# New costs in a planner's clock, constants and product order set anew, and the RG-LRU gate weights loaded once per layer: a two-layer hybrid diffusion backbone on one Trainium2 core

## The chip, the core and the metric

The kernel runs on one core of one Trainium2 chip, as one launch. The metric is the device time of that launch in microseconds, median of the runs. One execution was also taken by the hardware profiler; its span runs from the first to the last instruction. Engines in the rows: PE is TensorE (matmuls), PEld its weight loads, DVE is VectorE, ACT is ScalarE, POOL is GpSimd, SP is SyncE, which here only issues DMAs (SPq is its queue).

## What is computed

Two trunk layers over 128 context tokens and 512 latent tokens of width 1024, all fp32. Each layer is a modulated RMSNorm, one input projection that feeds three parallel mixers, an output projection, a second modulated RMSNorm and a gated MLP of width 2816. Cut to what matters here:

```python
def mixer(h, states, p, pos):
    proj = h @ p['w_in']                       # q k v g | z xbc dt | xl gl
    ...                                        # (A) retention, 6 heads, both directions
    xbc = jax.nn.silu(dwconv(xbc, ...))        # (B) Mamba-2 SSD, 6 heads, both directions
    dt_f = jax.nn.softplus(dt_raw + p['ssd_dt_bias'][0])
    ...
    xl = dwconv(xl, p['lru_conv_w'], p['lru_conv_b'])    # (C) RG-LRU, 256 channels
    def lru_dir(xd, d, h0):                    # d = 0 forwards, 1 backwards
        r = sigmoid(xb @ p['lru_w_a'][d] + b)  # block-diagonal gate weights
        i = sigmoid(xb @ p['lru_w_x'][d] + b)
        log_a = -LRU_C * r * softplus(-p['lru_lambda'][d])
        return rglru_scan(log_a, i * xd, h0)
    out = concatenate([y_ret, y_ssd, y_lru]) @ p['w_out']

def conv_ffn(h, p):
    u = dwconv(h @ p['ffn_w_up'], ...)         # width-3 depthwise
    val, gate = split(u, 2)
    return (silu(gate) * val) @ p['ffn_w_down']
```

The outputs are the tokens after a last RMSNorm and the final context states of the three scans.

## The kernel before

**Tiles.** The 640 tokens are five tiles of 128 (tile 0 is the context). The normalised input lies feature-major in `h_hi` and `h_lo`, 8 blocks of 128 features by 642 columns (two zero columns part context and latents). Each fp32 product is three passes over split operands: high by high, high by low, low by high (names `wh`, `wl` for the weight's parts). A feature-major unit is one weight tile of 128x1024 (`raw`, split by ACT into `wh` and by DVE or POOL into `wl`): 8 blocks by 3 passes by two column pieces of 258 and 384, 48 matmuls. Token-major sweeps (`v`, `q`, `k`, `z`, output and down projections) take units of 30 matmuls.

**Order.** Everything is written by one program that plays a scheduler while it emits. A main stream of jobs (the products, in the order of a string such as `'l0 v l1 c6 ...'`) runs beside cooperative threads (convolutions, scans, retention, SSD, norms, modulation). `Clock` holds an estimated time for each engine; `Engine.account` adds an estimated cost for each instruction as it is emitted; a thread is stepped when its inputs should be there by that clock. The estimate sets nothing but the order: each engine then executes its own list in that order, and waits on the chip for whatever is late. `TUNE` holds four sets of constants (mixer and MLP of layer 0, mixer and MLP of layer 1): the order string, `look` (how many weight units are split ahead of the product that takes them), `bias` (how early each kind of thread is stepped), `stages` (below) and others.

**The RG-LRU gates.** For each layer there are two channel blocks c and two directions d. `lru` loads the 128x2x128 gate weights of one (c, d) into a tile `wg` that has one buffer, and multiplies them by the convolved input `X`: two kinds (r and i), two pieces each, four fp32 matmuls `at<-X,wg`. So there are eight loads, and each one but the first of a layer must wait for the last matmul of the one before; the load stands in SP's queue wherever the thread came to it, often right behind the store of the last direction's state (`out_lru`), which waits for a DVE scan:

```python
            wg = fb.tile([128, 2, 128], F32, tag="wg", name="wg")
            SP.dma_start(wg, a["wlru"][l, c, :, d])
            yield 1
```

**Stages.** At the start of an MLP, and of layer 1's mixer, the first two or three units (`fm_primed`) run while the norm still turns the last tiles. They take the columns in parts: "A" is 0:258, 258:386, 386:642; "B" is 0:258, 258:642; "C" is 0:258, 258:514, 514:642.

**The start.** `start` loads x, norms it (ACT square and root, DVE reciprocal and scaling), transposes it on PE into PSUM, copies it into `xT`, while `setup` runs a softplus of some 25 small DVE instructions (`sp`, `lg`, `lam`, `e`); then `part` adds the bias to the first modulation's `rows`, PE transposes them, and `feats` scales `xT` and splits it into `h_hi` and `h_lo` for the first products.

Of the kernel before, what the change touches and what calls it, by code (L numbers as in the profile page):

```python
# [28 lines left out]
    {'look': 2, 'cap': 2.5, 'keep': 5, 'npr': 3, 'pmore': '', 'cf': 3, 'kz': 7, 'ke': 7, 'el': 5, 'order': 'l0 v l1 c6 c5 c3 c2 c4 q gl1 k z gl0', 'backlog': 4.9, 'slack': 1.53, 'lobias': 1.5, 'plag': 2.7, 'pbonus': 5.8, 'mkeep': 0, 'ng': 0, 'fine': 0, 'stages': 'B', 'bias': {'ret_chain': -0.2, 'ssd_run': 5.2, 'outs': 4.2, 'ret_tables': -3.6, 'ret_run': 4.4, 'rest': 2.0, 'ssd_chain': -2.1, 'dt_run': 2.8, 'states': 3.5, 'lru_run': 4.2}, 'klast': 1},  # L29
    {'look': 1, 'cap': 2, 'keep': 8, 'npr': 2, 'pmore': '0', 'cf': 3, 'kz': 5, 'ke': 8, 'el': 4, 'order': 'v l0 c2 c3 c4 c5 c6 l1 q k z gl0 gl1', 'backlog': 6.7, 'slack': 1.99, 'lobias': 0.6, 'plag': 0.7, 'pbonus': 1.5, 'mkeep': 0, 'ng': 0, 'fine': 0, 'stages': 'A', 'bias': {}, 'klast': 1},  # L30
    {'look': 2, 'cap': 2, 'keep': 3, 'npr': 3, 'pmore': '', 'cf': 2, 'kz': 3, 'ke': 8, 'el': 4, 'order': 'v l0 c2 c6 c5 c4 c3 l1 q z gl1 k gl0', 'backlog': 5.8, 'slack': 1.0, 'lobias': 1.6, 'plag': -1.0, 'pbonus': 3.8, 'mkeep': 0, 'ng': 0, 'fine': 0, 'stages': 'C', 'bias': {'ret_tables': -1.0, 'ret_run': -1.2, 'ssd_run': -2.7, 'ret_chain': 3.8, 'dt_run': 2.6, 'ssd_chain': -1.6, 'outs': 2.3, 'rest': -2.2, 'states': 0.2}, 'klast': 2},
    {'look': 1, 'cap': 1, 'keep': 8, 'npr': 3, 'pmore': '0', 'cf': 3, 'kz': 5, 'ke': 8, 'el': 4, 'order': 'v l0 c2 c3 c4 c5 c6 l1 q k z gl0 gl1', 'backlog': 5.6, 'slack': 0.49, 'lobias': 1.0, 'plag': 0.1, 'pbonus': 4.0, 'mkeep': 0, 'ng': 0, 'fine': 1, 'stages': 'C', 'bias': {}, 'klast': 1},
# [27 lines left out]
class Clock:  # L60
    """estimated times of the engines, for the order in which instructions are emitted"""

    def __init__(self):
        self.t = {k: 0.0 for k in ("PE", "ACT", "DVE", "POOL", "SP", "DMA")}
        self.ready, self.read, self.fin = {}, {}, 0.0
        self.table, self.dep, self.last = None, 0.0, 0.0
        self.cold, self.win, self.busy, self.rows = True, 0, 0.0, 1.0

# [11 lines left out]
    def add(self, eng, cost, lat, ins, outs):  # L80
# [30 lines left out]
    def free(self, n):  # L111
        """when the last user of a tile is done"""
# [18 lines left out]
ROWS = {"xT": NT, "s0": 2, "sh0": 2, "h_hi": NT, "h_lo": NT, "C456": 384}  # L131


def tnames(xs):
    """what the waits go by: tiles, or the rows of the tiles that are worked on in parts"""
    res = []
    for x in xs:
        n = getattr(getattr(x, "tensor", x), "name", None)
        w = ROWS.get(n.rsplit("_", 1)[0]) if n else None
        if w and not n.startswith(SHARED):  # L140
            ap = [(abs(st), c) for st, c in list(x.ap)[1:]]
            o = x.offset
            res += [f"{n}#{r}" for r in range(o // w, (o + sum(st * (c - 1) for st, c in ap)) // w + 1)]
        elif tname(x):
# [4 lines left out]
class Slots:  # L149
    """a pool whose tiles take over the waits of the tiles that had their place"""  # L150
# [16 lines left out]
class Engine:  # L167
# [13 lines left out]
    def account(self, fn, args, kw):  # L181
        def size(x):
            return int(np.prod([c for c in x.shape[1:]]))
# [10 lines left out]
        ns = sum(1 for x in aps[1:] if size(x) == 1 and n > 1)  # L194
        if self.key == "PE":
            f32 = args[1].dtype == F32
            cost = n * (4 if f32 and fn == "matmul" else 1) / 2400 + 0.003
# [15 lines left out]
        elif self.key == "DVE":  # L213
            if fn == "memset":
                return
            if fn == "tensor_scalar":
                cost = n / (960 if any(map(psum, ins)) else 1920) + 0.063 * (1 + ns)
            elif fn == "scalar_tensor_tensor":
                cost = n / 960 + 0.069 + 0.06 * ns
            elif fn == "reciprocal":  # L220
# [4 lines left out]
        elif self.key == "POOL":  # L225
            cost = 0.14 + n * 0.00216
            lat = 0.15
        else:
            b = n * 4 * out.shape[0] / 360e3
            start = max(c.t["SP"], c.dep)  # L230
            names = tnames(ins), tnames(outs)
            c.add("SP", 0.475, 0, *names)
            c.t["DMA"] = max(c.t["DMA"], c.t["SP"] + 0.65) + b
            for x in names[1]:
                c.ready[x] = (c.t["DMA"] + 1.0, "DMA")
            for x in names[0]:
                c.read.setdefault(x, {})["DMA"] = c.t["DMA"] + 1.0
            return
        c.add(self.key, cost, lat, tnames(ins), tnames(outs))
# [3 lines left out]
def kernel(ctx: ExitStack, tc: tile.TileContext, a: dict, o: dict):  # L243
# [27 lines left out]
    # PSUM tiles and token-major tiles are taken and given back in emission order, so that no engine waits for a later one  # L271
# [1637 lines left out]
```

## Time and profile before

| | us |
|---|---|
| median of three runs | 1764.8 |
| lowest, highest run | 1762.87, 1765.51 |
| span of the profiled execution | 1752.2 |
| median less span (launch and end, outside the span) | 12.6 |
| PE busy in the span | 1661.6 |
| DVE, ACT, POOL busy in the span | 1009.3, 718.5, 537.4 |

The profiler gives no other time for its own execution than the span, so that execution's time is the span and what lies around it, which the runs put at 12.6 us. Busy shares are averages over stages. A wait of an engine is put down in the rows to what was released last before it went on.

### The profile page before, as it was taken

The page shows a single profiled execution, that of the slowest core. Times are in us where ns is not written, and L with a number is a line of the kernel's source. Part 1 is how long each engine was busy: PE and PEld are TensorE (multiplying, and loading weights), DVE is VectorE, ACT ScalarE, POOL GpSimd, SP SyncE. Part 2 cuts the span into 40 slices and gives each one's busy share as a digit, 9 for nine tenths or more (in the row PEclk, how much of TensorE's full clock was granted, in tenths as well). Part 3 has the DMA queues.
Part 4 walks back from the last instruction along what each step waited for, and adds up shares of the span by engine and source line. Part 5 has one row for each costly group of instructions (what it writes and reads, how often), then busy time and mean ns, then how long its engine had stood idle before and what let it go on. Part 6 is the DMA issues. An engine that isn't in the chain of part 4 may idle for free.

```text
span 1752.2 us, 25505 instructions
## 1 busy us (share of the span) xinstructions
PE 1661.6 (95%) x10192; PEld 1485.5 (85%) x10192; DVE 1009.3 (58%) x1866; ACT 718.5 (41%) x1136; POOL 537.4 (31%) x344
## 2 busy tenths in 40 slices
PE   6897999999999999999999899999899999999997
PEld 5787878768997999799789876887799989998996
DVE  5467987677443344344464779877854434443445
ACT  6466435426332233223274765443453313331333
POOL 1334653322331233123123355442213212321331
PEclk9998999999999999999999999999999999999999
DMA  8424555533223222322533355643122321222222
GB/s 326 121 49 81 128 179 174 187 109 103 73 73 108 64 82 73 96 73 73 180 121 107 75 135 158 181 166 105 60 73 73 87 81 61 73 85 72 73 85 84
DMA packets 62668, 188.63 MB, mean 108 GB/s; under 512 B 9550, under 2 KB 17734, under 8 KB 62550
## 3 DMA queue, kind: packets, MB, share of 16 engines
q1 hardware_dynamic: 62550, 187.01, 34.7%
q8 instruction: 80, 1.31, 0.3%
q14 instruction: 38, 0.31, 0.1%
HBM read 180.46 MB, written 6.52 MB: 107 GB/s over the span
## 4 chain that ended last, share of the span: by engine, by line
PE 72%; DVE 14%; ACT 4%; DMA 4%; issue 3%; POOL 1%; SPq 0%; POOLq 0%; DVEq 0%; ACTq 0%
PE at L175 72%; DVE tok L175 5%; DVE x L175 2%; DMA wg<-in_wlru 2%; DVE gt L175 1%; DVE sp L175 1%; DVE C L175 1%; DMA tok<-cTd 1%; ACT L175 1%; DVE lb L175 1%; ACT xn L175 1%; ACT hf L175 1%; POOL wl L175 1%; DMA araw<-in_w_ada 1%; ACT lb L175 1%
## 5 line engine op out<-in xcount | busy, mean ns | idle before, releaser
L175 POOL TENSOR_TENSOR wl<-raw,wh 128x1024 fp32r<-128x1024 f32 (+3 forms) x167 | 388.3, 2326 | 946.7 <-ACT wh L175 883.2
L175 PE MATMUL at<-h_hi,wh 128*128 128x258 f32 (+2 forms) x1912 | 599.9, 314 | 5.0 <-ACT wh L175 3.9
L175 PE MATMUL at<-h_hi,wl 128*128 128x258 f32 (+2 forms) x1912 | 590.4, 309 | 5.6 <-POOL wl L175 4.8
L175 PE MATMUL at<-h_lo,wh 128*128 128x258 f32 (+2 forms) x1912 | 590.0, 309 | 0.5 <-DVE h_lo L175 0.5
L175 PEld LDWEIGHTS at<-h_hi,wh 128*128 128x128 f32 x1912 | 363.7, 190 | 20.1 <-issue 5.2
L175 PEld LDWEIGHTS at<-h_hi,wl 128*128 128x128 f32 x1912 | 362.8, 190 | 6.9 <-POOL wl L175 5.9
L175 PEld LDWEIGHTS at<-h_lo,wh 128*128 128x128 f32 x1912 | 364.1, 190 | 2.6 <-DVE h_lo L175 0.7
L175 ACT ACTIVATE wh<-raw 128x1024 fp32r<-128x1024 f32 (+3 forms) x210 | 212.7, 1013 | 223.1 <-PE at L175 168.1
L175 DVE SCALAR_TENSOR_TENSOR cv<-at,par,cv 128x258 f32<-128x258 f32 (+1 forms) x352 | 185.9, 550 | 71.4 <-ACT cv L175 59.6
L175 ACT ACTIVATE cv<-at,par 128x258 f32<-128x258 f32 (+1 forms) x130 | 76.5, 601 | 317.4 <-PE at L175 317.4
L175 PE MATMUL at<-wh,h_hi 128*128 128x384 f32 (+2 forms) x480 | 184.9, 385 | 2.3 <-DVE tok L175 1.4
L175 PE MATMUL at<-wl,h_hi 128*128 128x384 f32 (+2 forms) x480 | 172.6, 359 | 2.7 <-POOL wl L175 2.7
L175 PE MATMUL at<-wh,act_hi 128*128 128x512 f32 x440 | 174.3, 396 | 0.0
L175 PE MATMUL at<-wl,act_hi 128*128 128x512 f32 x440 | 173.6, 395 | 0.6 <-POOL wl L175 0.6
L175 PE MATMUL at<-wh,act_lo 128*128 128x512 f32 x440 | 173.4, 394 | 0.0
L175 PE MATMUL at<-wh,h_lo 128*128 128x384 f32 (+2 forms) x480 | 172.5, 359 | 0.0
L175 DVE TENSOR_SCALAR cv<-at,par 128x384 f32<-128x384 f32 x46 | 31.2, 677 | 188.3 <-PE at L175 188.3
L175 DVE TENSOR_TENSOR gt<-at,gate 128x512 f32<-128x512 f32 x100 | 68.4, 684 | 104.2 <-PE at L175 104.2
L175 ACT ACT_TABLE_LOAD x87 | 111.6, 1283 | 21.9 <-PE at L175 13.6
L175 PEld LDWEIGHTS at<-wh,h_hi 128*128 128x128 f32 x480 | 91.3, 190 | 28.4 <-issue 12.6
L175 PEld LDWEIGHTS at<-wh,act_hi 128*128 128x128 f32 x440 | 82.7, 188 | 24.0 <-issue 3.4
L175 PEld LDWEIGHTS at<-wl,h_hi 128*128 128x128 f32 x480 | 91.2, 190 | 12.2 <-POOL wl L175 3.5
(169 smaller groups left out, 1903.1 us busy)
## 6 DMA issues: line engine op xcount, KB each, us to landing
raw<-in_wup SPq DMA_DIRECT2D x88, 512.0 KB, 3.5
araw<-in_w_ada SPq DMA_DIRECT2D x80, 512.0 KB, 4.5
raw<-in_wdn SPq DMA_DIRECT2D x44, 512.0 KB, 3.5
raw<-in_wfm SPq DMA_DIRECT2D x28, 512.0 KB, 3.6
ar<-in_wada SPq DMA_DIRECT2D x16, 512.0 KB, 10.2
tok<-cTd SPq DMA_DIRECT2D x40, 192.0 KB, 4.6
raw<-in_wout SPq DMA_DIRECT2D x14, 512.0 KB, 3.5
x<-in_xin SPq DMA_DIRECT2D x10, 512.0 KB
```

Of the source, the lines that this page charges most:

```text
L175: res = real(*args, **kw)
```

## The change

It has five parts.

1. **Clock and costs.** Matmul costs, DVE's scan and the landing of a DMA get other numbers; tiles that many threads share (`h_hi`, `h_lo`, `act_hi`, `act_lo`) are now tracked by rows and blocks of columns; and DVE and POOL instructions that both read SBUF take turns in the clock (`port`). None of this emits an instruction; it changes the order.
2. **Constants.** All four sets of `TUNE`. Among them: `stages` C to A for layer 1's mixer, A to B and C to B for the MLPs; `look` 2 to 1 for layer 1's mixer and 1 to 2 for the last MLP; `lobias` down in the last MLP, which moves low-part splits from POOL to DVE.
3. **Product order** of both mixers (`v` first in layer 0; `z` ahead of `k`).
4. **Gate weights.** `wg` is one tile of 128x2x2x2x128 per layer, loaded by two DMAs when the pool `fb` is opened.
5. Comments and docstrings go.

```diff
-    {'look': 2, ..., 'order': 'l0 v l1 c6 c5 c3 c2 c4 q gl1 k z gl0', ..., 'stages': 'B', ...},
+    {'look': 2, ..., 'order': 'v l0 l1 c6 c5 c4 c3 c2 q z k gl1 gl0', ..., 'stages': 'B', ...},
...
+    def port(self, eng, start, cost):
+        other = self.held["POOL" if eng == "DVE" else "DVE"]
+        for a, b in other:
+            if a <= start < b:
+                start = b
+        mine = self.held[eng]
+        mine.append((start, start + cost))
+        if len(mine) > 24:
+            del mine[0]
+        return start
...
+        if port:
+            start = self.port(eng, start, cost)
...
-ROWS = {"xT": NT, "s0": 2, "sh0": 2, "h_hi": NT, "h_lo": NT, "C456": 384}
+ROWS = {"xT": NT, "s0": 2, "sh0": 2, "h_hi": NT, "h_lo": NT, "act_hi": NT, "act_lo": NT, "C456": 384}
...
             if fn == "transpose":
                 cost = 0.109
-            tp = kw.get("tile_position")
-            if tp is not None and tp[1] > 0:
-                cost = 0.02
+            elif args[1].dtype != F32:
+                cost = max(0.112, 0.0055 + 0.000443 * n)
+            elif tp is not None:
+                cost = 0.108 if args[1].shape[1] == 64 else 0.32 if n == 512 else 0.1
+            else:
+                cost = 2 * max(0.111, 0.00084 * n)
...
+            land = c.t["DMA"] + (3.4 if wide else 1.4)
             for x in names[1]:
-                c.ready[x] = (c.t["DMA"] + 1.0, "DMA")
+                c.ready[x] = (land, "DMA")
...
         for d in range(2):
             gates = []
-            wg = fb.tile([128, 2, 128], F32, tag="wg", name="wg")
-            SP.dma_start(wg, a["wlru"][l, c, :, d])
+            wg = mods["wg", l][:, c, d]
             yield 1
...
         def lru_run(c):
-            while c > len(st["lru"]):
+            while c > len(st["lru"]) or ("wg", l) not in mods:
                 yield
...
                     pl.enter("fb", f"fb{l}")
+                    wg = mods["wg", l] = pl["fb"].tile([128, 2, 2, 2, 128], F32, tag="wg", name="wg")
+                    for c in range(2):
+                        SP.dma_start(wg[:, c], a["wlru"][l, c])
                     S["C456"] = pl["fb"].tile([128, 3 * NT], F32, tag="C456", name="C456")
```

What this does to the engines' lists, at three places. First SP's queue in layer 0's mixer (each row a DMA, tile<-source, width; `raw` is a weight unit, `araw` a modulation unit). Before:

```order
L175 DMA wg<-in_wlru 128x256
L175 DMA raw<-in_wfm 128x1024 x2
L175 DMA out_lru<-Y 128x1
L175 DMA wg<-in_wlru 128x256
L175 DMA raw<-in_wfm 128x1024
L175 DMA rows<-in_bada 128x512
```

After, from the last loads of the start on:

```order
L195 DMA raw<-in_wvd 128x780 x3
L195 DMA araw<-in_w_ada 128x1024 x2
L195 DMA wg<-in_wlru 128x512 x2
L195 DMA pv<-in_sssd 128x192 x4
L195 DMA raw<-in_wvd 128x780
L195 DMA raw<-in_wfm 128x1024 x4
```

The loads of `wg` no longer stand behind `out_lru`; both of the layer stand ahead of the state loads `pv` and of the fourth `v` unit, and no load of `wg` follows in that mixer. The four groups of gate products move later: on PE, 78 main matmuls now stand between the end of `v` and the product of the log-decays `la`, where in layer 1 there were 66.

Second, PE at the start of layer 0's MLP, around the last modulation unit (`araw`) between two stages. Before:

```order
L175 MATMUL at<-h_hi,wh 128x128
L175 MATMUL at<-h_lo,wh 128x128
L175 MATMUL at<-h_hi,wl 128x128
L175 MATMUL at<-araw,csil 32x512 x4
L175 MATMUL at<-h_hi,wh 128x256
L175 MATMUL at<-h_lo,wh 128x256
L175 MATMUL at<-h_hi,wl 128x256
```

After:

```order
L195 MATMUL at<-h_hi,wh 128x258
L195 MATMUL at<-h_lo,wh 128x258
L195 MATMUL at<-h_hi,wl 128x258
L195 MATMUL at<-araw,csil 32x512 x4
L195 MATMUL at<-h_hi,wh 128x384
L195 MATMUL at<-h_lo,wh 128x384
L195 MATMUL at<-h_hi,wl 128x384
```

Pairs of a 128 and a 256 columns wide matmul have become one of 384. Over the three stage plans 120 such pairs go (48 here, 72 in the last MLP); layer 1's mixer keeps its pairs in another order.

Third, DVE in the start. Before:

```order
L175 RECIPROCAL rs<-ss 128x1
L175 TENSOR_SCALAR x<-x,rs 128x1024
L175 TENSOR_SCALAR sp_149<-sp_148 128x32
L175 RECIPROCAL sp_149<-sp_149 128x32
L175 TENSOR_TENSOR sp_148<-sp_148,sp_149 128x32
```

After:

```order
L195 TENSOR_SCALAR x<-x,rs 128x1024
L195 TENSOR_SCALAR spi<-par 128x32
L195 COPY xT<-at 128x4x128 x5
L195 TENSOR_SCALAR sp_184<-sp_183 128x32
L195 RECIPROCAL sp_184<-sp_184 128x32
L195 TENSOR_TENSOR sp_183<-sp_183,sp_184 128x32
```

Five of the ten copies of the turned x have come from ACT to DVE, ahead of the softplus chain. Further on, 39 more low-part splits of a weight (`wl`) are on DVE than before and as many fewer on POOL: 40 more in the last MLP, two more in the first, three fewer in the mixers.

## Rows read from the trace of the kernel before

**Rows 1.** The page's first part: each engine's busy time, share of the span, instructions.

```profile
PE 1661.6 (95%) x10192; PEld 1485.5 (85%) x10192; DVE 1009.3 (58%) x1866; ACT 718.5 (41%) x1136; POOL 537.4 (31%) x344
```

**Rows 2.** Busy by stretch: length, PE, PEld, DVE, ACT, POOL (instructions), granted clock, DMA share, GB/s.

```profile
412.00:870.00 458.00, 458.00 (x2781) 421.91 (x2782) 203.31 (x320) 141.19 (x192) 113.89 (x49) 1.00 0.29 93
```

**Rows 3.** PE's timeline, gate products: start, length, operation, [idle before it, releaser].

```profile
84.78 2.48 PE L175 MATMUL at<-X,wg 128*128 128x258 f32 x4 [6.94 <-DMA wg<-in_wlru]
152.29 3.98 PE L175 MATMUL at<-X,wg 128*128 128x258 f32 x7 [11.07 <-DMA wg<-in_wlru]
991.17 2.48 PE L175 MATMUL at<-X,wg 128*128 128x258 f32 x4 [6.14 <-DVE tok L175]
1033.83 1.32 PE L175 MATMUL at<-X,wg 128*128 128x258 f32 x4 [3.19 <-DMA wg<-in_wlru]
1060.59 2.48 PE L175 MATMUL at<-X,wg 128*128 128x258 f32 x4 [3.75 <-DVE tok L175]
```

**Rows 4.** The chain that ended last, two loads of wg: start, length.

```profile
141.69 10.46 DMA wg<-in_wlru
...
1025.49 8.20 DMA wg<-in_wlru
```

**Rows 5.** SP's timeline, the load of wg ahead of the product at 991.17.

```profile
983.50 0.38 SPq L175 DMA_DIRECT2D wg<-in_wlru  x1
```

**Rows 6.** DVE's timeline, the instruction that ended as PE went on at 991.17.

```profile
990.78 0.28 DVE L175 TENSOR_SCALAR tok<-cst,dt 128x128 f32<-128x128 f32 x1
```

**Rows 7.** Busy by stretch, as rows 2: during gate waits and just after.

```profile
84.80:90.00 5.20, 5.20 (x13) 4.21 (x14) 0.00 (x0) 1.62 (x4) 0.00 (x0) 0.50 0.30 104
...
141.20:152.30 11.10, 0.03 (x2) 0.04 (x1) 5.95 (x14) 5.06 (x5) 2.80 (x1) 0.65 0.76 38
152.30:158.30 6.00, 6.00 (x15) 4.42 (x16) 0.00 (x0) 2.87 (x6) 0.70 (x1) 0.51 0.22 82
...
985.00:991.20 6.20, 0.06 (x2) 0.06 (x1) 5.91 (x14) 2.17 (x3) 0.96 (x1) 0.71 0.55 38
991.20:994.50 3.30, 3.30 (x9) 2.51 (x10) 1.34 (x5) 1.27 (x3) 0.00 (x0) 0.50 0.54 201
1056.80:1060.60 3.80, 0.05 (x2) 0.04 (x1) 3.73 (x11) 0.01 (x1) 2.74 (x3) 0.83 1.25 46
1060.60:1066.20 5.60, 5.60 (x13) 4.40 (x14) 3.53 (x11) 1.38 (x3) 1.65 (x1) 0.50 0.83 314
```

**Rows 8.** PE's timeline, first and last of runs 256 and 128 columns wide, at full clock.

```profile
907.10 0.28 PE L175 MATMUL at<-h_lo,wh 128*128 128x256 f32 x1
...
912.60 0.28 PE L175 MATMUL at<-h_hi,wl 128*128 128x256 f32 x1
...
912.88 0.28 PE L175 MATMUL at<-h_hi,wl 128*128 128x128 f32 x1
...
915.34 0.28 PE L175 MATMUL at<-h_hi,wh 128*128 128x128 f32 x1
```

**Rows 9.** The same for a run of 384 columns, first and last of 40.

```profile
159.16 0.34 PE L175 MATMUL at<-wh,h_hi 128*128 128x384 f32 x1
...
165.99 0.34 PE L175 MATMUL at<-wh,h_hi 128*128 128x384 f32 x1
```

**Rows 10.** PE's timeline, layer 1's product of the log-decays.

```profile
952.74 0.85 PE L175 MATMUL at<-la,cst 128*128 128x60 f32 x6 [2.12 <-DVE la L175]
```

**Rows 11.** ACT's timeline of the start, the ten copies of the turned x.

```profile
15.00 4.97 ACT L175 ACTIVATE xT<-at 128x512 f32<-128x512 f32 x10
```

**Rows 12.** DVE's timeline of the start, in the softplus chain.

```profile
20.98 2.39 DVE L175 TENSOR_SCALAR lam<-spo 128x8 f32<-128x8 f32 x2
```

**Rows 13.** POOL's timeline of the start.

```profile
20.98 2.37 POOL L175 TENSOR_TENSOR wl<-raw,wh 128x1024 fp32r<-128x1024 f32 x1 [20.54 <-ACT wh L175]
```

**Rows 14.** Groups by form: count, busy us, mean ns of one, idle before and its releasers.

```profile
L175 ACT ACTIVATE wh<-raw 128x1024 fp32r<-128x1024 f32 x174 | 183.3, 1053 | 207.8 <-PE at L175 160.4 <-DVE x L175 36.5 <-issue 5.8
...
L175 DVE TENSOR_TENSOR wl<-raw,wh 128x1024 fp32r<-128x1024 f32 x37 | 45.3, 1224 | 79.1 <-ACT wh L175 78.3
```

More of the change, by code (lines that the diff above doesn't have):

```diff
@@ L33 @@
+    {'look': 2, 'cap': 0.5, 'keep': 8, 'npr': 3, 'pmore': '0', 'cf': 3, 'kz': 5, 'ke': 8, 'el': 4, 'order': 'v l0 c2 c3 c4 c5 c6 l1 q k z gl0 gl1', 'backlog': 6.5, 'slack': -0.22, 'lobias': 0.39, 'plag': -3.5, 'pbonus': 4.0, 'mkeep': 0, 'ng': 0, 'fine': 0, 'stages': 'B', 'bias': {'dt_run': -0.4, 'load_gate': -0.5, 'ret_tables': 2.4, 'feats': 0.7, 'rest': -0.5, 'lru_fin': -2.8, 'norm_thread': -1.9, 'part': -2.2}, 'klast': 1},
 ]
@@ L67, in __init__ @@
         self.cold, self.win, self.busy, self.rows = True, 0, 0.0, 1.0
+        self.held = {"DVE": [], "POOL": []}
     def now(self):
@@ L139, in tnames @@
         w = ROWS.get(n.rsplit("_", 1)[0]) if n else None
-        if w and not n.startswith(SHARED):
+        if w:
             ap = [(abs(st), c) for st, c in list(x.ap)[1:]]
             o = x.offset
-            res += [f"{n}#{r}" for r in range(o // w, (o + sum(st * (c - 1) for st, c in ap)) // w + 1)]
-        elif tname(x):
+            rows = range(o // w, (o + sum(st * (c - 1) for st, c in ap)) // w + 1)
+            if n.startswith(SHARED):
+                c0, cn = o % w, sum(st * (c - 1) for st, c in ap if st < w) + 1
+                res += [f"{n}#{r}#{b}" for r in rows for b in range(c0 // 64, (c0 + cn - 1) // 64 + 1)]
+            else:
+                res += [f"{n}#{r}" for r in rows]
+        elif n:
             res.append(n)
@@ L194, in account @@
         ns = sum(1 for x in aps[1:] if size(x) == 1 and n > 1)
+        port = False
         if self.key == "PE":
[L196 to L197 removed]
+            tp = kw.get("tile_position")
             if fn == "transpose":
                 cost = 0.109
[L200 to L202 removed]
+            elif args[1].dtype != F32:
+                cost = max(0.112, 0.0055 + 0.000443 * n)
+            elif tp is not None:
+                cost = 0.108 if args[1].shape[1] == 64 else 0.32 if n == 512 else 0.1
+            else:
+                cost = 2 * max(0.111, 0.00084 * n)
             lat = 0.2
@@ L215, in account @@
                 return
+            wide = [x for x in ins if size(x) > 1 or n == 1]
+            port = not any(map(psum, ins)) and not (fn in ("tensor_reduce", "reciprocal"))
             if fn == "tensor_scalar":
@@ L227, in account @@
             lat = 0.15
+            port = True
         else:
             b = n * 4 * out.shape[0] / 360e3
-            start = max(c.t["SP"], c.dep)
             names = tnames(ins), tnames(outs)
             c.add("SP", 0.475, 0, *names)
+            wide = n * out.shape[0] > 3 * int(np.prod([k[1] for k in ins[0].ap if k[0]]))
             c.t["DMA"] = max(c.t["DMA"], c.t["SP"] + 0.65) + b
+            land = c.t["DMA"] + (3.4 if wide else 1.4)
             for x in names[1]:
-                c.ready[x] = (c.t["DMA"] + 1.0, "DMA")
+                c.ready[x] = (land, "DMA")
             for x in names[0]:
-                c.read.setdefault(x, {})["DMA"] = c.t["DMA"] + 1.0
+                c.read.setdefault(x, {})["DMA"] = land
             return
-        c.add(self.key, cost, lat, tnames(ins), tnames(outs))
+        c.add(self.key, cost, lat, tnames(ins), tnames(outs), port)
 @with_exitstack
```

13 lines of the change are left out of this document (7 added, 6 removed).

## The prediction

> **What bounds the kernel now.** I read the page's busy times first. PE is busy 1661.6 us [rows 1] of a span of 1752.2, so only 1752.2 - 1661.6 = 90.6 us are PE idle, and time can come from two places: that idle time, and what PE's busy time costs (instructions and clock). The table of stretches comes next: in the middle of layer 0's MLP PE is busy 458.00 of 458.00 us at a granted clock of 1.00, while DVE has 203.31 us of work and POOL 113.89 [rows 2]. In such a stretch nothing that DVE, ACT or POOL do has a price as long as it stays covered. So the idle time is in the start, the mixers and the turns between stages.
>
> PE's timeline of the mixers shows the largest single item: the product of the RG-LRU gates waits for 6.94, 11.07, 6.14, 3.19 and 3.75 us [rows 3], together 31.1 us, a third of all idle time. Three of the five are put down to the load of `wg`. Two are put down to a DVE instruction, `tok`. I take these for the load too. The chain of waits has two other loads of `wg`, which took 10.46 and 8.20 us to land [rows 4]. The load ahead of the wait that ends at 991.17 was issued at 983.50 [rows 5], 7.7 us earlier, which is about a landing, and the DVE instruction that ends then, at 991.06 [rows 6], writes a tile that the gate product doesn't read. But in that stretch DVE was busy 5.91 of 6.20 us, and in the other 3.73 of 3.80 [rows 7]. So whoever takes the load away may find DVE's own queue behind it.
>
> The wait also costs time after it. In the stretches that follow four of the waits PE is busy throughout at a granted clock of 0.50 or 0.51, its lower level of 1.2 GHz, for 5.20, 6.00, 3.30 and 5.60 us [rows 7]. At 2.4 GHz that work takes half: 20.1 / 2 = 10.05 us lost.
>
> **The change part by part.** *Gate weights.* The load is issued when the pool opens and the gate products come later in the list, so a landing of 8 to 10 us [rows 4] is covered by the loads' lead, tens of microseconds of `v` units. Of the waits that are clearly the load's, 6.94 + 11.07 + 3.19 = 21.2 us go [rows 3], and with the first two (5.20 + 6.00) / 2 = 5.6 us of half clock [rows 7]: 26.8. For the two behind which DVE is busy, 6.14 + 3.75 = 9.9 us of wait [rows 3] and (3.30 + 5.60) / 2 = 4.45 of clock [rows 7], 14.3 together, the bounds are 0 and 14.3. DVE's work there isn't what the product reads, but PE's next products may be waiting on it, so I take half, 7.2. On SP the loads go ahead of the state loads and one `v` unit: two issues of some 0.4 us [rows 5], covered by units that are already loaded. Sum: -34.0.
>
> *Stages.* 120 pairs of 128 and 256 columns become one matmul of 384. Between 907.10 and 912.60 lie 46 steps of the wider kind, 0.1196 us each; between 912.88 and 915.34 lie 22 of the narrower, 0.1118 [rows 8]. The 384 columns wide take (165.99 - 159.16) / 39 = 0.1751 us [rows 9]. A pair saves 0.1196 + 0.1118 - 0.1751 = 0.0563 us, and 120 of them 6.8. Fewer, wider parts ask for their columns of `h` sooner, which could turn into a wait for the norm; bounds 0 to -6.8, and I take all of it, because PE works there without a break.
>
> *Log-decays.* In layer 1 the product of `la` waits 2.12 us for DVE [rows 10]. Twelve more main matmuls stand ahead of it; between 0.1196 [rows 8] and 0.1751 us [rows 9], 0.147 in the mean, these are 1.8 us. -1.8, bounds 0 and -2.12.
>
> *Start.* Ten copies of `xT` take ACT 4.97 us [rows 11], 0.50 each. Five of them now stand ahead of the softplus chain on DVE, which delays that chain, and the addition to `rows` and the first products behind it, by about 5 x 0.50 = 2.5 us; the least is nothing, if ACT, rid of five copies, brings `feats` forward by as much. I take +2.5. The chain has another price: its two `lam`, 128x8 each, took 2.39 us together [rows 12], against 2.37 of the POOL split that began at the same moment [rows 13]: DVE stood while POOL ran. *Here a rule of the Trainium skill bears (page "SBUF — State Buffer", section "SBUF: two separate sides"): VectorE and GpSimd share one port pair as an exclusive lock, and whoever comes second is blocked for the whole instruction of the other. This row agrees, 2.39 beside 2.37. By the rule a softplus chain that starts later lies beside two POOL splits instead of one, so the start would cost 2.5 + 2.4 = 4.9 and not 2.5; the sum would be 2.4 longer.* The upper end that I keep for the start is two copies' worth and a split more than the middle: 2.5 + 2.37 + 1.0 = 5.9 from [rows 11, 13].
>
> *Order, constants, clock.* These emit nothing. 40 splits more on DVE in the last MLP, at 1.224 us [rows 14], are 49 us of DVE, while an MLP stretch of 458 us leaves DVE 254.7 us idle [rows 2]: nothing, and were that cover gone, up to 49. The two new product orders keep each unit's work. They gather side work (gates, log-decays, chains) at the end of layer 0's mixer, so PE can meet a wait that isn't there now. No row shows it. Below it is nothing, above it is as much as the largest wait beside busy DVE, 6.14 [rows 3]; I take about half, +3.
>
> **Sum.** -34.0 - 6.8 - 1.8 + 2.5 + 3 = -37.1. The profiled span becomes 1715.1, and with the 12.6 us that the runs put around it 1727.7. The profiled execution and the 12.6 stand for the median by construction, so this is 1764.8 - 37.1.
>
> **The rivals.** *All of it comes back.* The waits named after DVE are the load's alone, the start gains on ACT what it loses on DVE, and no new wait comes: -26.8 - 14.3 - 6.8 - 2.1 = -50.0, so 1714.8. For it: the operand argument on `tok` [rows 5, 6]. Against it: a list that loses 30 us of waits has always something next in line.
>
> *DVE becomes the bound of the mixers.* Then the stalls give back only what DVE itself stood idle in them: of the second 11.10 - 5.95 = 5.15, of two others 0.29 and 0.07 [rows 7], of the first at most its 6.94 [rows 3], 12.5 together, and the clock still falls behind them. With the stages and both costs: -12.5 - 6.8 + 2.5 + 3 = -13.8, so 1751.0. For it: DVE's share of those stretches. Against it: over the whole span DVE is busy 1009.3 us, 58% [rows 1], so it can catch up as soon as PE has other work.
>
> *The change doesn't do what it says.* The gate products wait as long for another operand (the convolved `X`, or a free PSUM tile), and only the stages pay: -6.8 + 2.5 + 3 = -1.3, so 1763.5. Against it: three of five waits carry the load's name [rows 3].
>
> *Slower: one unit ahead in layer 1's mixer.* With `look` 1 a unit's split begins when the unit before it starts. A unit of 30 matmuls of 0.1751 lasts 5.25 us [rows 9]; ACT's part of the split takes 1.05 [rows 14] and POOL's 2.37 [rows 13], which leaves 1.8 us for everything else in ACT's and POOL's queues. Where these hold the split up for more, PE waits at each unit. There are 39 units (30 in the mixer, 9 in the output projection): at 37.1 / 39 = 0.95 us each beyond that slack the gain is gone, and at 1.4 each the time is 1764.8 - 37.1 + 54.6 = 1782.3. For it: ACT and POOL carry the side threads too; the ten copies above hold ACT 4.97 us in one stretch [rows 11], more than that slack. Against it: it must happen at nearly all units, and layer 1's mixer has no such row now.
>
> **How the numbers follow.** The sum 0.48; all comes back 0.20; DVE the bound 0.18; no effect 0.04; slower 0.10. The likeliest case's own range is 1715 to 1743: below, the whole of the 14.3, no cost of start and order and the rest as it is; above, none of the 14.3 (+7.2), start +3.4, order +3.1 and log-decays +1.8, 15.5 in all. The range that should hold 8 in 10 takes in the two neighbours, 1706 to 1754, and leaves out the last two cases and some of the tails. A difference under 0.2%, 3.5 us, is about what a measurement of this kernel can't tell from none. Faster than that: 0.48 + 0.20 + 0.18 = 0.86; the case without effect is within it, 0.04; slower 0.10.
>
> **What would show it right or wrong.** In the trace after, no gate product should have an idle time of more than a microsecond before it, and no stretch at a clock of 0.50 of several microseconds should follow one; the loads of `wg` should land long before. The stages should show matmuls of 384 columns where pairs of 128 and 256 stood, and PE's busy time should be down by some 15 us: 6.8 of matmuls and 5.6 to 10 of clock. `rows` should come 2 to 3 us later in the start. If instead PE waits for DVE in the same places, with DVE busy throughout, DVE is the bound; if waits for `wh` or `wl` come in each unit of layer 1's mixer, it is the slower case. The prediction fails altogether if the sum of PE's idle time doesn't fall below 70 us.

## The result and the profile after

The changed kernel takes 1741.2 us, median of 4 runs (1738.86 to 1742.58), against 1765.15 of the kernel before: ratio 0.987, 95% interval 0.9856 to 0.9884, so 1.2 to 1.4% less. That is 23.9 us less, where the sum had 37.1. The profiled execution's span is 1738.5 us, 13.7 less than the 1752.2 of before. Between a run's time and its span lie 1.8 us (1740.3 and 1738.5 in the profiled one). So the 12.6 us that the prediction read as launch and end were for the greater part something else: the profiled execution of before, 1752.2 + 1.8 = 1754.0 us, was some 9 us shorter than the shortest of the four runs. On the three chips of the experiments the kernel before took 1757.8, 1758.9 and 1759.2 us, which is why every experiment below is read against the runs of before on its own chip. Because of this the traces are compared with a second profile of before as well, called c_before here, of 1754.8 us.

The first part of the page of the changed kernel, to be held against [rows 1]:

```profile
span 1738.5 us, 25216 instructions
...
PE 1665.1 (96%) x10072; PEld 1485.3 (85%) x10072; DVE 1068.3 (61%) x1908; ACT 708.7 (41%) x1130; POOL 445.8 (26%) x308
```

PE's idle time went from 90.6 to 73.4 us, but PE's busy time did not fall by the 15 us that were expected: it rose from 1661.6 to 1665.1. PE's timeline shows the gate products, to be held against [rows 3]; all others of them start without a wait of 0.4 us or more:

```profile
144.45 0.70 PE L195 MATMUL at<-X,wg 128*128 128x258 f32 x2 [1.55 <-DVE C L195]
146.28 1.65 PE L195 MATMUL at<-X,wg 128*128 128x384 f32 x2 [1.13 <-DVE C L195]
...
1057.81 1.32 PE L195 MATMUL at<-X,wg 128*128 128x258 f32 x4 [2.07 <-DVE tok L195]
```

No wait is the load's any more: SP issued the loads of layer 0 at 50.17 and 50.59 us and the first gate product started at 91.46. But PE waits at other places. PE's timeline of the changed kernel at the start, at the entry of layer 0's MLP, in layer 1's mixer, in its output projection and at the entry of the last MLP:

```profile
29.79 0.47 PE L195 MATMUL at<-ident,rows 128*128 128x128 f32 x1 [6.01 <-DVE rows L195]
...
395.53 0.58 PE L195 MATMUL at<-h_hi,wh 128*128 128x258 f32 x1 [2.76 <-ACT h_hi L195]
...
400.79 1.97 PE L195 MATMUL at<-ident,xn 128*128 128x128 f32 x8 [1.45 <-ACT xn L195]
...
1130.11 1.79 PE L195 MATMUL at<-tok 128*128 128x64 f32 x12 [1.60 <-DVE tok L195]
...
1220.03 0.50 PE L195 MATMUL at<-wh,h_hi 128*128 128x512 f32 x1 [2.89 <-ACT wh L195]
1222.52 0.79 PE L195 MATMUL at<-wl,h_hi 128*128 128x512 f32 x1 [1.98 <-POOL wl L195]
1225.29 0.79 PE L195 MATMUL at<-wl,h_hi 128*128 128x512 f32 x1 [1.12 <-POOL wl L195]
1228.87 0.87 PE L195 MATMUL at<-ident,tok 128*128 128x128 f32 x3 [2.36 <-DVE tok L195]
...
1262.18 1.97 PE L195 MATMUL at<-ident,xn 128*128 128x128 f32 x8 [5.34 <-ACT xn L195]
```

The waits at 395.53, 400.79 and 1130.11 are new. The first, in the start, was 5.55 us for ACT at the same product before. In the output projection and at the entry of the last MLP the kernel before has 1.92, 1.99 and 3.62 us, 7.5 together; the five rows of the changed kernel there are 13.7.

Three stretches of the changed kernel, with columns as in [rows 2], to be held against [rows 7]:

```profile
395.50:405.00 9.50, 7.52 (x32) 6.93 (x33) 6.02 (x11) 8.71 (x19) 1.75 (x2) 0.50 0.29 116
1222.50:1235.00 12.50, 9.00 (x22) 6.27 (x23) 9.82 (x16) 0.82 (x2) 2.73 (x1) 0.51 0.29 85
1132.00:1136.00 4.00, 4.00 (x26) 3.50 (x24) 3.81 (x12) 1.20 (x1) 0.00 (x0) 0.57 0.02 4
```

The lower clock of 1.2 GHz is there again, behind the new waits. I sum PE's busy time times (1 - granted clock) over stretches of 1 us in which the clock is below 0.985: 18.4 us are lost so in the first profile of before and 20.7 in c_before, 23.3 in the changed kernel and 20.7 in a second profile of it; so two profiles of one kernel differ by 2.3 and 2.6 us. The 5.6 to 10 us of clock that the sum gave back did not come back.

By stages, c_before and then the second profile of the changed kernel (c_after, span 1736.9). The stages are: start and layer 0's mixer, its output projection, its MLP, layer 1's mixer with output projection, the last MLP with the end.

```profile
0.00:330.14 330.14, 287.62 (x1995) 250.87 (x1996) 230.18 (x519) 177.72 (x297) 129.74 (x114) 0.95 0.48 145
330.14:404.94 74.80, 70.59 (x328) 52.39 (x327) 54.45 (x93) 27.05 (x54) 18.68 (x11) 0.98 0.43 151
404.94:893.24 488.30, 486.22 (x2930) 445.10 (x2928) 226.89 (x359) 160.66 (x234) 121.11 (x52) 1.00 0.29 93
893.24:1263.94 370.70, 342.93 (x2077) 292.49 (x2076) 269.25 (x539) 192.34 (x329) 149.32 (x120) 0.97 0.43 124
1263.94:1754.80 490.86, 476.23 (x2870) 445.62 (x2868) 228.77 (x360) 160.93 (x227) 117.86 (x49) 0.99 0.25 78
```

```profile
0.00:313.89 313.89, 284.88 (x1992) 247.22 (x1992) 230.49 (x514) 177.52 (x299) 133.78 (x115) 0.98 0.54 162
313.89:387.73 73.84, 69.88 (x330) 53.67 (x328) 52.05 (x92) 22.36 (x40) 19.62 (x12) 0.98 0.28 100
387.73:884.09 496.36, 490.18 (x2881) 445.98 (x2880) 239.86 (x376) 155.52 (x229) 119.56 (x52) 0.99 0.29 93
884.09:1251.97 367.88, 346.60 (x2085) 295.06 (x2084) 270.41 (x537) 196.75 (x338) 150.44 (x121) 0.97 0.41 125
1251.97:1736.90 484.93, 470.11 (x2790) 440.03 (x2788) 277.43 (x393) 156.71 (x226) 23.39 (x11) 0.99 0.25 79
```

From length to length: -16.3, -1.0, +8.1, -2.8 and -5.9, together -17.9. Nearly all of the gain is layer 0's mixer, layer 0's MLP gives half of it back, and layer 1's mixer, from which the sum took some 12 us (3.19 and 7.2 of gate waits, 1.8 of log-decays), gave 3.

### The profile page after: what moved, and what is told of

Same layout as the page of the kernel before. It is cut to its first block, busy times and chain, and to the rows that moved or that the text cites. A ratio compares the mean times of both kernels' runs of the same rounds, so it can differ in the third digit from the quotient of the medians.

```text
span 1738.5 us, 25216 instructions
## 1 busy us (share of the span) xinstructions
PE 1665.1 (96%) x10072; PEld 1485.3 (85%) x10072; DVE 1068.3 (61%) x1908; ACT 708.7 (41%) x1130; POOL 445.8 (26%) x308
## 4 chain that ended last, share of the span: by engine, by line
PE 79%; DVE 11%; ACT 3%; DMA 3%; issue 3%; POOL 1%; SPq 0%; POOLq 0%; DVEq 0%; ACTq 0%
PE at L195 79%; DVE tok L195 3%; DVE x L195 2%; DMA tok<-cTd 2%; DVE sp L195 2%; DVE gt L195 1%; DMA araw<-in_w_ada 1%; ACT xn L195 1%; ACT hf L195 1%; DVE C L195 0%; DVE h_lo L195 0%; ACT h_hi L195 0%; POOL wl L195 0%; SPq L195 0%; DVE mu L195 0%
## 5 line engine op out<-in xcount | busy, mean ns | idle before, releaser
L195 PE MATMUL at<-h_hi,wh 128*128 128x258 f32 (+2 forms) x1872 | 589.8, 315 | 3.2 <-ACT h_hi L195 3.1
L195 PE MATMUL at<-h_hi,wl 128*128 128x258 f32 (+2 forms) x1872 | 581.9, 311 | 2.0 <-POOL wl L195 1.9
L195 PE MATMUL at<-h_lo,wh 128*128 128x258 f32 (+2 forms) x1872 | 582.1, 311 | 0.8 <-DVE h_lo L195 0.8
L195 POOL TENSOR_TENSOR wl<-raw,wh 128x1024 fp32r<-128x1024 f32 (+3 forms) x128 | 292.9, 2289 | 1064.0 <-ACT wh L195 1044.4
L195 PEld LDWEIGHTS at<-h_hi,wh 128*128 128x128 f32 x1872 | 356.6, 191 | 21.2 <-ACT h_hi L195 4.8
L195 PEld LDWEIGHTS at<-h_lo,wh 128*128 128x128 f32 x1872 | 356.9, 191 | 2.7 <-DVE h_lo L195 1.3
L195 PEld LDWEIGHTS at<-h_hi,wl 128*128 128x128 f32 x1872 | 355.8, 190 | 2.4 <-POOL wl L195 2.4
L195 ACT ACTIVATE cv<-at,par 128x258 f32<-128x258 f32 (+1 forms) x113 | 64.4, 587 | 295.8 <-PE at L195 295.7
L195 DVE TENSOR_TENSOR wl<-raw,wh 128x1024 fp32r<-128x1024 f32 (+1 forms) x82 | 100.6, 1227 | 137.3 <-ACT wh L195 136.6
L195 DVE TENSOR_SCALAR cv<-at,par 128x384 f32<-128x384 f32 x63 | 42.7, 677 | 149.7 <-PE at L195 149.7
```

Source lines behind the costliest of these rows:

```text
L195: res = real(*args, **kw)
```

## The experiments

All ratios are to the kernel before on the same chip, in 4 to 15 runs of each kernel.

**The loads alone, written by the scheduler.** The kernel before with part 4 of the change and nothing else (e1_loads_only).

```diff
-            wg = fb.tile([128, 2, 128], F32, tag="wg", name="wg")
-            SP.dma_start(wg, a["wlru"][l, c, :, d])
+            wg = mods["wg", l][:, c, d]
...
                     pl.enter("fb", f"fb{l}")
+                    wg = mods["wg", l] = pl["fb"].tile([128, 2, 2, 2, 128], F32, tag="wg", name="wg")
+                    for c in range(2):
+                        SP.dma_start(wg[:, c], a["wlru"][l, c])
```

> The kernel before, with the gate weights alone changed: one tile per layer, two loads when the pool opens; clock, constants, product order and stages stay. First theory (the five waits before the gate products belong to the load, as the sum had it): 26.8 us for the three waits named after the load and their half clock, and between 0 and 14.3 for the two named after DVE, so 1724 to 1738 us, with no gate product waiting over 1 us. Rival (DVE's queue stands behind the load): only what DVE itself was idle comes back, about 12.5 us, so near 1752, and the waits at the gate products remain under DVE's name. If neither the place nor the length of these waits changes: 1765.

Measured: 1777.4 us, ratio 1.0102 (1.0089 to 1.0115): 20 us **more**. Neither theory had that. The gate waits did go (the longest left at a gate product is 2.03 us). But the scheduler plays on from another number at each load, and it wrote another mixer. In layer 0 six waits follow one another, on PE's timeline:

```profile
310.46 2.98 PE L175 MATMUL at<-araw,csil 128*32 128x512 f32 x8 [2.67 <-DMA araw<-in_w_ada]
316.43 1.87 PE L175 MATMUL at<-araw,csil 128*32 128x512 f32 x4 [2.99 <-DMA araw<-in_w_ada]
...
331.00 0.87 PE L175 MATMUL at<-ident,tok 128*128 128x128 f32 x3 [3.69 <-DVE tok L175]
345.67 2.82 PE L175 MATMUL at<-xs,tok 128*128 128x64 f32 x12 [5.63 <-DVE tok L175]
```

The modulation units and the chunk work stand at the end of the mixer without main products between them. So this kernel tests the loads together with a new order, and can't tell the two apart.

**The old constants under the new clock** (e2_old_constants).

```diff
 TUNE = [
-    {'look': 2, 'cap': 2.5, 'keep': 5, ..., 'order': 'v l0 l1 c6 c5 c4 c3 c2 q z k gl1 gl0', ...},
+    {'look': 2, 'cap': 2.5, 'keep': 5, ..., 'order': 'l0 v l1 c6 c5 c3 c2 c4 q gl1 k z gl0', ...},
...
```

> The changed kernel (new clock and costs, gate weights ahead) with the constants of before: order strings, stages, look, lobias, bias. First theory (the gate weights bring nearly all, the new constants little, since what they save in stage matmuls they lose at the start of layer 0's MLP and in layer 1's mixer): 1735 to 1746 us, that is within 6 us of the changed kernel. Rival (constants and clock belong together, and the old constants under the new clock put threads at wrong places): 1750 to 1770, with new waits of several us in the mixers.

Measured: 1781.3 us, ratio 1.0136 (1.0118 to 1.0155). The rival holds, and by more than it said: the same kind of waits (5.04, 3.08, 4.47, 3.84 and 4.59 us at modulation, chunk and `k` products, and 5.94 at the entry of layer 0's MLP) cost more than the loads bring. The constants belong to one clock.

**Stages A again in layer 0's MLP** (e3_mlp0_stages_A).

```diff
-    {'look': 1, 'cap': 1.5, ..., 'stages': 'B', ...},
+    {'look': 1, 'cap': 1.5, ..., 'stages': 'A', ...},
```

> The changed kernel with stages A again in layer 0's MLP alone (tiles 0 and 1, then tile 2, then tiles 3 and 4). First theory (the wider part of stages B asks for the last tiles of the norm before they are turned, and PE falls to its lower clock behind that wait): the waits of 2.8 and 1.5 us near 395 and 400 us and some 3.5 us of half clock go, 48 pairs of matmuls cost 2.7 us more: 1736 us, 5 less. Rival (the norm itself is later in the new order, so that the third part waits as long as the second did): 1741 to 1744, with the wait at the last part.

Measured: 1740.5 us, ratio 0.990 (0.9887 to 0.9914), not below the changed kernel's 0.987. PE's timeline has the same two waits at the same products:

```profile
390.62 0.58 PE L195 MATMUL at<-h_hi,wh 128*128 128x258 f32 x1 [2.75 <-ACT h_hi L195]
...
395.88 1.97 PE L195 MATMUL at<-ident,xn 128*128 128x128 f32 x8 [1.45 <-ACT xn L195]
```

The first theory falls. The wait stands at the first part (258 columns, the same in A and B), not at the wide one: it is the norm's own turn through ACT that is late.

**Look 2 again in layer 1's mixer** (e4_look2).

```diff
-    {'look': 1, 'cap': 2, 'keep': 2, ..., 'order': 'v l0 c5 c2 c4 c6 l1 c3 q z gl0 k gl1', ...},
+    {'look': 2, 'cap': 2, 'keep': 2, ..., 'order': 'v l0 c5 c2 c4 c6 l1 c3 q z gl0 k gl1', ...},
```

> The changed kernel with look 2 again in layer 1's mixer. First theory (with one unit ahead ACT's and POOL's parts of a split come too late once side work fills these engines): the waits for wh and wl at the end of the output projection, 2.9 + 2.0 + 1.1 us, and the 4.4 us lost there at the lower clock go: about 1731 us. Rival (these waits belong to the burst of norm and retention work at the end of the output projection, not to look): they stay, 1738 to 1744. Second rival: what is split earlier holds ACT and POOL while the mixer's threads want them, and the time goes up, 1745 to 1752.

Measured: 1766.1 us, ratio 1.0048 (1.0036 to 1.0061), some 31 us over the changed kernel's 0.987 on that chip. The waits for `wh` did go, but the mixer was written anew, with waits of 4.83, 3.92, 3.80, 6.10 and 3.04 us between 1072 and 1190 us. The second rival had this direction, at less than half the size. Again an order was tested, not `look`.

**The order held fast.** In e5 to e8 an edit is made so that the clock counts the old instructions at their old place, while the new ones are emitted without being counted. Every engine's list is then the same, row for row, but for the edit. (In e9 and e10 `look` changes, and the order is written anew behind that point.) First the kernel before with the loads ahead (e5_ahead_same_order):

```diff
-            wg = fb.tile([128, 2, 128], F32, tag="wg", name="wg")
-            SP.dma_start(wg, a["wlru"][l, c, :, d])
+            sw, was = Stand(f"wg_{l}{c}{d}", (128, 2, 128)), fb.names.setdefault("wg", [])
...
+            SP.account("dma_start", (sw, a["wlru"][l, c, :, d]), {})
+            wg = mods["wg", l][:, c, d]
...
+                    wg = mods["wg", l] = pl["fb"].real.tile([128, 2, 2, 2, 128], F32, tag="wgs", name="wgs", bufs=1)
+                    for c in range(2):
+                        SP.real.dma_start(wg[:, c], a["wlru"][l, c])
```

> The kernel before with the gate weights loaded ahead, and with every other instruction of every engine in the order that it has in the kernel before: the clock still counts the eight old loads where they stood, and the two new ones are emitted without being counted. First theory (the waits are the load's, and the plain loads-only kernel was slower because the scheduler, which plays on from another number, wrote a worse order): 27 to 41 us less than before, ratio 0.977 to 0.985, no wait of over 1 us at a gate product. Rival (the loads only hid other waits of the same length, which the loads-only kernel showed under the names of DVE and the modulation's DMA): at most 12 us less, ratio 0.993 to 1.000.

Then the changed kernel with eight single loads in its own order (e6_single_same_order), the same edit the other way round:

```diff
-            wg = mods["wg", l][:, c, d]
+            wg = fb.real.tile([128, 2, 128], F32, tag="wgs", name="wgs", bufs=1)
+            SP.real.dma_start(wg, a["wlru"][l, c, :, d])
```

> The changed kernel with the eight loads of before, each at its place in the thread and with one buffer, and every other instruction in the order of the changed kernel. First theory (the loads ahead are worth in the new order what the sum said): the waits at the gate products come back, 20 to 40 us more than the changed kernel. Rival (in the new order the gate products stand apart and later, so that even single loads land in time): within 5 us of the changed kernel, and the gain came from the order.

and the changed kernel itself beside them (c_after):

> The changed kernel itself, beside the others on one chip, since chips differ by some tenths of a per cent. Both theories expect the ratio to before that was measured, 0.987.

| | single loads | loads ahead |
|---|---|---|
| order of before | 1758.9 us (before) | 1738.5, ratio 0.9886 (0.9868 to 0.9904) |
| order of the changed kernel | 1770.6, ratio 1.0060 (1.0045 to 1.0075) | 1738.4, ratio 0.9874 (0.9857 to 0.9892) |

The loads ahead are worth 20.4 us in the old order and 32.2 in the new one. The rest of the change (clock, constants, product orders, stages) costs 11.8 us with single loads and nothing that can be measured with loads ahead. So the gain is that of the gate weights, and it is between the two theories of e5: more than 12 us, less than 27. In e6 the first theory holds, and the waits are back, here the first and third of four on PE's timeline (the others are 3.38 and 6.70 us):

```profile
114.70 1.20 PE L836 MATMUL at<-X,wgs 128*128 128x258 f32 x2 [7.84 <-DMA wgs<-in_wlru]
...
997.60 1.20 PE L836 MATMUL at<-X,wgs 128*128 128x258 f32 x2 [4.61 <-DMA wgs<-in_wlru]
```

In e5 the five waits for gate weights, 31.0 us in c_before, are gone but for 0.88 us, at the product that was the last of [rows 3]:

```profile
1036.52 0.67 PE L811 MATMUL at<-X,wgs 128*128 128x258 f32 x2 [0.88 <-DVE tok L182]
```

What took the place of the waits is on PE's timeline of e5, five that are new or, as the second, longer than they were (1.97 us in c_before):

```profile
136.72 0.62 PE L811 MATMUL at<-X,wgs 128*128 128x384 f32 x1 [2.69 <-DVE C L182]
...
164.82 0.90 PE L182 MATMUL at<-ident,C 128*128 128x128 f32 x3 [4.17 <-ACT xs L182]
...
1013.41 1.06 PE L811 MATMUL at<-X,wgs 128*128 128x258 f32 x3 [2.81 <-ACT lb L182]
...
1053.65 0.55 PE L182 MATMUL at<-ident,tok 128*128 128x128 f32 x3 [2.32 <-DVE C L182]
...
1077.46 1.07 PE L182 MATMUL at<-araw,csil 128*32 128x512 f32 x2 [3.80 <-DMA araw<-in_w_ada]
```

Busy by stretch around the last of them:

```profile
1075.00:1084.00 9.00, 6.54 (x26) 4.88 (x27) 4.72 (x8) 3.23 (x8) 2.96 (x3) 0.62 0.79 143
```

Its stages of layer 0's mixer (15 us shorter than in c_before) and of layer 1's mixer with output projection (3 us shorter):

```profile
0.00:315.52 315.52, 285.29 (x1995) 250.28 (x1996) 232.93 (x519) 177.50 (x297) 128.81 (x114) 0.98 0.50 152
...
878.40:1245.69 367.29, 343.97 (x2077) 292.16 (x2076) 269.27 (x539) 191.56 (x329) 149.50 (x120) 0.97 0.43 125
```

In layer 1 the three waits were 12.8 us in c_before, and the idle time of this stage fell only from 370.70 - 342.93 = 27.8 to 367.29 - 343.97 = 23.3.

Over the whole span PE is idle 74.0 us in e5 and 91.2 in c_before, and the lower clock takes 20.2 and 20.7. In the new order it is otherwise: PE is idle 95.4 us in e6 and 75.2 in c_after, and the lower clock takes 28.7 and 20.7. So in the new order the time at the lower clock went with the gate waits, by 8.0 us; in the old order the 0.5 us between e5 and c_before is less than two profiles of one kernel differ.

**The softplus chain behind the first modulation** (e7_setup_late), in the order of the changed kernel.

```diff
-        spawn(setup(), 0)
+        late = []
+        g = held(setup(), late)
...
+            if q == 3:
+                for real, args, kw in late:
+                    real(*args, **kw)
```

> The changed kernel with the softplus chain of the start (42 small instructions of DVE and ACT) emitted behind the last of the four parts of the first modulation, all else in the same order. First theory (the chain, with two POOL splits that hold it for 2.4 and 2.3 us, is what the first products wait for): the first product starts 5 to 8 us earlier, and the time falls by 4 to 8 us against the changed kernel. Rival (the first products then wait for the loads of the modulation's weights, which are issued up to 25.7 us): the first product moves by 1 to 3 us, and the time by no more than 2.

Measured: 1741.7 us, ratio 0.9896 (0.988 to 0.9913), against 0.9874 of the changed kernel beside it: not faster. The first product starts at 31.89 instead of 34.34 us in the first profile of the changed kernel, 2.5 us earlier, as the rival had it: `rows` is added 10 us earlier, but PE's list holds the next modulation product ahead of the transpose, and that waits 4.74 us for its load. The chain on ACT then holds up a weight split, 4.13 us at 55.04:

```profile
24.45 2.27 PE L214 MATMUL at<-ar,csil 128*32 128x128 f32 x32 [4.74 <-DMA ar<-in_wada]
...
55.04 0.69 PE L214 MATMUL at<-wh,h_hi 128*128 128x390 f32 x1 [4.13 <-ACT wh L214]
```

**The kernel before, once more** (c_before).

> The kernel before itself, with a second profile, on the chip of the three runs beside it. First theory (its profiled execution was a fast one, and waits on DMAs make its length vary): the span lies some us above the first profile's 1752.2, near the median of the runs less 1.8 us, with longer waits at the loads of the gate weights or elsewhere. Rival (the profile is typical, and the difference is between chips): the same waits to within 0.5 us, a span within 2 us of 1752.

Measured: 1758.6 us, ratio 0.9996, span 1754.8, 2.6 above the first profile. The waits at the gate products are the same to within 1 us. One row matters: the wait near 991 that was named after `tok` in [rows 3] is named after the load here. Whether the first profile's execution was a short one by chance or ran on a faster chip is not shown.

```profile
990.17 1.20 PE L175 MATMUL at<-X,wg 128*128 128x258 f32 x2 [5.65 <-DMA wg<-in_wlru]
```

**The copies of the start on ACT** (e8_copies_on_act), all else in the same order.

```diff
-                    DVE.tensor_copy(dst, src)
+                    ACT.real.activation(dst, src, AF.Copy)
+                    DVE.account("tensor_copy", (dst, src), {})
```

> The changed kernel with all ten copies of the turned x on ACT again, every other instruction in the same order on its engine. First theory (the five copies on DVE put the softplus chain 3 us later, and so beside two POOL splits instead of one): the chain meets one split, the first product starts 4 to 5 us earlier, and the time falls by 3 to 5 us against the changed kernel, ratio to before 0.984 to 0.986. Rival (with the copies back on ACT the weight splits come later, so that the first products wait for them, or the start's gain is taken up by a later load): within 2 us of the changed kernel.

**Look 2 from layer 1's output projection on** (e9_look2_out); everything ahead of it is unchanged.

```diff
         job([], lambda: need((l, 1)))
+        if l == 1:
+            hook(lambda: setattr(tn, "look", 2))
```

> The changed kernel with look 2 from layer 1's output projection on (until the last MLP, which has 2 anyway); all instructions before that point stay as they are. First theory (one unit ahead is too little there: ACT stands 8 us behind one retention tile, and the last splits of the weights with it): the waits of 2.9, 2.0 and 1.1 us and most of the 4.3 us of half clock go, 6 to 9 us less than the changed kernel, ratio 0.982 to 0.984. Rival (the waits are for the retention tile itself, which DVE and POOL deliver late): PE waits for the tile in place of the splits, within 3 us of the changed kernel.

**Both** (e10_both).

> The changed kernel with both edits: the copies of the start on ACT, and look 2 from layer 1's output projection on. First theory: the two gains lie in different stages and add, 9 to 14 us less than the changed kernel, ratio 0.979 to 0.982. Rival: what the start gains is given back before the output projection, so that it equals the kernel with look 2 alone.

Measured: ratios 0.9864 (0.9848 to 0.9879), 0.9862 (0.9844 to 0.9881) and 0.9863 (0.9847 to 0.9879), that is 1736.5, 1736.9 and 1736.6 us, against 1736 to 1737 that the two ratios of the changed kernel give on that chip. None is apart from the changed kernel, and the two don't add. In e8 the first theory falls. Without the copies the chain on DVE waits 1.84 us for `sp` from ACT, a wait that the copies had covered, and so it goes on only 0.7 us earlier (18.25 in place of 18.96 us). POOL's splits, whose `wh` ACT now makes behind all ten copies, begin 2.8 us later (24.12 in place of 21.32) and meet the chain at its last eight instructions. These take 1.15 us in the changed kernel. The first product starts 0.6 us earlier, at 33.75, and not 4 to 5. DVE's timeline of the changed kernel, then DVE's and POOL's of e8:

```profile
28.39 1.15 DVE L195 TENSOR_SCALAR e<-lg,par 128x6 f32<-128x6 f32 x8
```

```profile
18.25 0.18 DVE L195 TENSOR_SCALAR sp<-sp 128x32 f32<-128x32 f32 x1 [1.84 <-ACT sp L195]
...
23.39 5.45 DVE L195 TENSOR_SCALAR e<-lg,par 128x6 f32<-128x6 f32 x8
```

```profile
24.12 4.69 POOL L195 TENSOR_TENSOR wl<-raw,wh 128x1024 fp32r<-128x1024 f32 x2 [23.68 <-ACT wh L195]
```

In e9 the waits of 2.89, 1.98, 1.12 and 2.36 us become two of 1.22 and 1.87, and the entry of the last MLP waits 2.49 and 2.22 us instead of 5.34. But PE now waits earlier, and the lower clock comes with it, 0.53 over 14.5 us:

```profile
1189.55 0.86 PE L195 MATMUL at<-ident,rows 128*128 128x128 f32 x3 [2.71 <-DVE rows L195]
```

```profile
1189.50:1204.00 14.50, 14.45 (x77) 13.23 (x77) 9.69 (x23) 1.12 (x3) 2.43 (x5) 0.53 0.01 2
```

## Why the prediction was right, and where its sum was not

The direction and the cause were right, and 1741.2 lies in the likeliest case's own range of 1715 to 1743. That it does is in part luck: the range's upper end was added up from other misses than those that came. By its own signs the prediction did worse. It called itself failed altogether if PE's idle time did not fall below 70 us, and that time is 73.4 (75.2 in c_after). PE's busy time was to fall by some 15 us; it rose by 3.5, and from c_before to c_after it fell by 1.9. No gate product was to wait over 1 us, and three wait 1.13 to 2.07. `rows` was to be added 2 to 3 us later and was added 5.1 us later (29.45 in place of 24.35). The sum had 37.1 us of gain where 23.9 came, 13.2 too many, and these are the terms.

*Gate weights, -34.0.* The mechanism is shown: with the order held fast the loads bring 20.4 us, and taking them back costs 32.2. That the two waits named after DVE were the load's is shown too, for the first by c_before's row at 990.17 and for both by e5, where nothing is left of the first and 0.88 us of the second. The size is off, 20.4 in place of 34.0, for two reasons. The 5.6 us of half clock, and the half of 4.45, were counted as given back with the waits; but e5 loses 20.2 us to the lower clock, c_before 20.7. The lower clock is found again around waits that came in their place, as the 0.62 around 1077.46 shows. And the step "of the waits that are clearly the load's, 21.2 us go" let nothing stand behind them: in e5 the five waits of 2.3 to 4.2 us shown above, 15.8 together, stand where the stalls had covered all but some 2 us of them. The half that I took for DVE's queue was put on the two waits named after DVE, and these went; what came back stands at other products, and behind all five.

*Stages, -6.8.* The last MLP is 5.9 us shorter in c_after than in c_before, with 72 pairs gone (4.1 by the sum). In layer 0's MLP nothing of the other 2.7 can be seen, in a stage that has become longer (next term). PE's busy time over the whole span, less what the lower clock took of it, is 1644.1 us in e3, which has these 48 pairs again, and 1641.0 in c_after and 1641.8 in the changed kernel. But for the kernel before it is 1642.9 in c_before and 1643.2 in the first profile. So it fell by 1.9 and 1.4 us only, and where the rest of the 6.8 went is not shown.

*Order and constants, +3, and the upper end of 6.* This is a term that was too small: with the loads ahead, all of the change but the gate weights is worth nothing that can be measured, where the sum had -3.1 for it. Layer 0's MLP is 8.1 us longer: 490.18 of 496.36 us busy against 486.22 of 488.30, so 4.1 us more idle, and some 4 lost at the lower clock around 395 to 405. e3 shows that stages B aren't the cause; what made the norm's turn late on ACT was not tried. In layer 1 the output projection's three waits for splits are the price of `look` 1 that the slower rival named, at 3 units and not at 39, and in e9, without it and with another order there, as much time is lost elsewhere.

*Start, +2.5, upper end 5.9.* The first product started at 28.63 us before and starts at 34.34, 5.7 later (6.5 from c_before to c_after). Here the rule of the Trainium skill (page "SBUF — State Buffer", section "SBUF: two separate sides") gave the better number, 4.9. The chain on DVE, 0.18 to 0.19 us an instruction, lies beside two POOL splits, and two of its instructions take a split's time. DVE's timeline, then POOL's, to be held against [rows 12, 13]:

```profile
21.34 2.38 DVE L195 TENSOR_SCALAR sp<-sp 128x32 f32<-128x32 f32 x1
23.76 2.27 DVE L195 TENSOR_TENSOR sp<-sp,sp 128x32 f32<-128x32 f32 x1
```

```profile
21.32 4.66 POOL L195 TENSOR_TENSOR wl<-raw,wh 128x1024 fp32r<-128x1024 f32 x2 [20.89 <-ACT wh L195]
```

The five copies took 3.08 us, a little more than the 2.5; but e8 shows that the chain without them goes on only 0.7 us earlier, since it waits for ACT. What the later start costs in the end is not shown: e7 and e8 brought the first product 2.5 and 0.6 us forward, and neither is faster than the changed kernel.

*Log-decays, -1.8.* PE waits 0.40 us in layer 1 where it waited 2.12, so -1.7.

*The frame.* The sum was made on a profiled execution that was some 10 us shorter than the runs shown, and the difference was called launch and end. It is 1.8 us. By profiles alone the change is -13.7 or, with the second profiles of both, -17.9; by runs it is -23.9, and -20.5 on the chip of c_after.

Of the rivals, "all of it comes back" was right on the two waits named after DVE and is refuted by the new waits of e5, and "no effect" is refuted by e5 and e6. "DVE the bound" is right in part: the new waits are for DVE, ACT and one load, whichever came next, not for DVE throughout.

## What to carry to other kernels

Where a program that plays a scheduler writes the order, an edit tested by itself tests a new order too: hold the order fast, by counting the old instruction and emitting the new one, before saying what the edit is worth. A removed wait gives back what lies between it and the next late thing, here 20 of 34 us, and the time at the lower clock need not fall with it: 20.7 and 20.2 us in the old order. A wait named after an engine whose instruction doesn't touch the product's operands is worth a second profile: the name can change.

## What the runs showed that was not expected

Waits much shorter than those of [rows 3] were followed by the lower clock, but not each time. After 1.60 us of waiting at 1130.11, in a stretch of products of 64 columns, the granted clock was 0.57 over 4 us in which PE was busy throughout. In e9, whose instructions are in the same order up to there, the same product waited the same 1.60 us at 1128.96, and the clock stayed at 1.00:

```profile
1130.00:1138.00 8.00, 8.00 (x65) 6.58 (x65) 6.81 (x17) 6.19 (x11) 2.92 (x3) 1.00 0.22 59
```

What made the difference is not shown. And a small DVE instruction of 0.18 us was held as long as the POOL split beside it, 2.27 and 2.38 us in the changed kernel. Where the splits met the chain at another place (e8), they still cost DVE 4.3 us, 5.45 in place of 1.15.
